# Attention scores and values of two feature tiles side by side in a gated decoder block

## The chip, the cores and the metric

One core of a Trainium2 chip runs one launch of the kernel. The metric is the device time of a launch in microseconds; lower is better. Before the change it is 444.75 us (median of three runs, 444.67 to 445.67).

## What is computed

The reference is one decoder block on 256 tokens of width 1024, in float32. Two mixers run beside each other on the same normalised input and are added with sigmoid gates; then come an output projection, a squared-ReLU MLP, a gated embedding and a final norm. The change touches only the attention mixer, which with 256 tokens and blocks of 256 is plain causal attention with a relative bias (cut to what matters):

```python
h = rms_norm(x, norm_mix_g[i])
za_u, za_v, q, k, v_att, g_a, g_b = jnp.split(h @ w_in[i], offsets, axis=-1)
y_a = sgu_mixer(jax.nn.gelu(za_u), jax.nn.gelu(za_v), ...)
s_own = jnp.einsum('bhqd,bhmd->bhqm', q_c, k_own) * scale + table[:, rel_bucket(dist_own)]
probs = jax.nn.softmax(jnp.where(dist_own >= 0, s_own, -jnp.inf))
y_b = jnp.einsum('bhqm,bhmd->bhqd', probs, v_own)        # 16 heads of 64 features
merged = jax.nn.sigmoid(g_a) * y_a + jax.nn.sigmoid(g_b) * y_b
x = x + merged @ w_out[i]
```

## The kernel before

Activations lie with features on the 128 partitions, in eight feature tiles of 128; a feature tile c holds the two heads 2c and 2c+1 (64 partitions each). All weights come as 53 tiles of 1 MB in one fixed order (`ORDER`, line 34). Each weight tile is split by two engines: ScalarE writes the rounded high part (`hi`, line 84), VectorE the remainder (`lo`, line 85). A projection is then three matmuls per 128x128 block (lines 117 to 119: hi with the high and the low half of the activations, lo with the high half), each 128x128 stationary and 256 columns moving. Of `hi` and `lo` there are three buffers each, and of the raw tiles four; `weights()` splits two tiles ahead of the one it hands out, so a tile is split while the two before it are used.

The schedule is by hand: each engine runs its instructions in the order in which the program issues them. The stretch around the change is the loop over J (two turns). A turn handles four feature tiles c to c+3 and eight weight tiles: keys for two tiles (`keys`, w_in 12+), attention's v (`proj_tok`, two w_va tiles), and the two sigmoid gates for two pairs of tiles (`proj_h(20..)` and `proj_h(24..)`, with `gate_tanh`). A projection is done in two halves of 24 matmuls, and its `mid` hook puts other TensorE work between the halves. The attention work per feature tile is:

- scores (lines 396 and 399): four matmuls, the two heads at once, each on 64 of the 128 rows of the array (tile 64x128), 256 or 128 columns. They are in full float32, so the chip runs each as two passes, and the profile counts eight.
- softmax: VectorE scales and adds the bias (lines 401, 403) and finds the maxima (line 407), ScalarE takes the exponentials (line 411). `att_normalise` (lines 418, 421) is VectorE's.
- `att_transpose` (line 430): six 128x128 transposes on TensorE, copied to `pt` by ScalarE (line 431).
- values (lines 441, 442): four matmuls, the two heads at once, each on 64 of the 128 columns of the array (tile 128x64), two passes each.
- when both tiles of a pair are done, `merge` (lines 451 to 454 on VectorE, then `split_act`: line 107 on ScalarE, line 108 on VectorE).

In the program before, every score tile and every value tile is put into the stream of projections at a place of its own: eight places for scores and eight for values, all with matmuls of 128x128 in front and behind. PSUM has one bank for `yb` (values), two buffers of two banks for scores, and three banks (`mm`) for projections and transposes together.

```python
        keys(b, mid=lambda: att_scores(c))
...
        ta[a] = gate_tanh(proj_h(20, a, transpose_and_score(c, c + 2)), f"ta{a}")
        att_normalise(c + 2)
        att_values(c)
        tb[a] = gate_tanh(proj_h(24, a, transpose_and_score(c + 1, c + 3)), f"tb{a}")
```

Of the kernel before, what the change touches and what calls it, by code (L numbers as in the profile page):

```python
# [10 lines left out]
F32 = mybir.dt.float32  # L11
# [5 lines left out]
P = 128  # L17
# [33 lines left out]
def block_kernel(ctx: ExitStack, tc: tile.TileContext, xt, xk, pt, rows, wst, bsp, rel, buckets, wts, out):  # L51
# [7 lines left out]
    scores = tc.tile_pool(name="scores", bufs=2, space=bass.MemoryType.PSUM)  # L59
    ps_scores = scores.__enter__()  # L60
# [34 lines left out]
    def weights(key, width, ahead=3):  # L95
        i = POS[key]
        split_to(i + ahead)
        k = 2048 // width
        return (hi[i].rearrange("p (k c) -> p k c", k=k), lo[i].rearrange("p (k c) -> p k c", k=k))


    def pair_tile(tag, name, k=KD):
        return act.tile([P, k, 2, S], F32R, tag=tag, name=name)
# [17 lines left out]
    def tok3(os_, x, wh, wl, first, last):  # L121

        ts = [slice(t * P, (t + 1) * P) for t in range(2)]
        for t in range(2):
            nc.tensor.matmul(os_[t], x[:, 0, ts[t]], wh, start=first, stop=False)  # L125
        for t in range(2):
            nc.tensor.matmul(os_[t], x[:, 0, ts[t]], wl, start=False, stop=False)  # L127
            nc.tensor.matmul(os_[t], x[:, 1, ts[t]], wh, start=False, stop=last)  # L128

    def halves(c):  # L130
        return slice(c * 512, (c + 1) * 512)

    def bank(tag="mm", bufs=3, shape=(P, 2, 256)):
        return ps.tile(list(shape), F32, tag=tag, name=f"{tag}_t", bufs=bufs)
# [80 lines left out]
    def proj_T(key, x, mid=None, ahead=3):  # L215

        wh, wl = weights(key, CW, ahead)
        o = bank()
        for f in range(2):
            fs = slice(f * P, (f + 1) * P)  # L220
            for k in range(KD):
                mm3(o[:, f], wh[:, k, fs], wl[:, k, fs], x[:, k], k == 0, k == KD - 1)
            if f == 0 and mid:
                mid()
        return o

    def proj_tok(name, c, x, mid=None):

        os_ = [bank(shape=(P, 512)) for t in range(2)]
        for i in range(2):  # L230
            wh, wl = weights((name, 2 * c + i), 512)
            for k in range(4):
                tok3(os_, x[:, 4 * i + k], wh[:, k], wl[:, k], i + k == 0, i == 1 and k == 3)
            if i == 0 and mid:
                mid()
        return os_
# [58 lines left out]
    hT = pair_tile("xA", "hT")  # L295
# [30 lines left out]
    o = proj_T(("w_in", 0), xg2, ahead=2)  # L326
# [4 lines left out]
    o = proj_T(("w_in", 1), xg2, ahead=2)  # L331
# [3 lines left out]
    o = proj_T(("w_in", 2), xg2, ahead=2)  # L335
# [3 lines left out]
    o = proj_T(("w_in", 3), xg2)  # L339
# [19 lines left out]
    def by_half(a):  # L359
        return a.rearrange("p c (t s) -> p (c t) s", t=2)  # L360
# [18 lines left out]
    for j in range(4):  # L379
        o = proj_T(("w_in", 8 + j), hT)  # L380
# [5 lines left out]

    va = act.tile([P, 2, D], F32, tag="t8a", name="va")
    mT = pair_tile("xB", "mT")
    sc_sb, pt_sb, yb = {}, {}, {}
    parts = (slice(0, 256), slice(256, 384))  # L390

    def att_scores(c):
        sp = ps_scores.tile([P, 2, 512], F32, tag="scores", name=f"sp{c}")
        for h in range(2):
            rs = slice(h * DH, (h + 1) * DH)
            nc.tensor.matmul(sp[:, h, 0:256], qT[rs, c, P:2 * P], kT[rs, c], start=True, stop=True)  # L396
        for h in range(2):
            rs = slice(h * DH, (h + 1) * DH)
            nc.tensor.matmul(sp[:, h, 256:384], qT[rs, c, 0:P], kT[rs, c, 0:P], start=True, stop=True)
        s = tmp.tile([P, 2, RVW], F32, tag="s", name=f"s{c}", bufs=3)  # L400
        nc.vector.scalar_tensor_tensor(s[:, :, 0:256], sp[:, :, 0:256], DH ** -0.5,
                                       TB[:, 2 * c:2 * c + 2, :], op0=OP.mult, op1=OP.add)
        nc.vector.scalar_tensor_tensor(s[:, :, 256:384], sp[:, :, 256:384], DH ** -0.5,
                                       TB[:, 2 * c:2 * c + 2, P:2 * P], op0=OP.mult, op1=OP.add)
        nm = small.tile([P, 2, 2], F32, tag="nm", name=f"nm{c}")
        for i, cs in enumerate(parts):
            nc.vector.tensor_reduce(nm[:, i], s[:, :, cs], axis=AX.X, op=OP.max, negate=True)  # L407
        sm = small.tile([P, 2, 2], F32, tag="sm", name=f"sm{c}")
        for i, cs in enumerate(parts):
            for h in range(2):  # L410
                nc.scalar.activation(s[:, h, cs], s[:, h, cs], AF.Exp, bias=nm[:, i, h:h + 1],  # L411
                                     accum_out=sm[:, i, h:h + 1])
        sc_sb[c] = (s, sm)

    def att_normalise(c):
        s, sm = sc_sb[c]
        rc = small.tile([P, 2, 2], F32, tag="rc", name=f"rc{c}")
        nc.vector.reciprocal(rc, sm)
        for i, cs in enumerate(parts):
            for h in range(2):  # L420
                nc.vector.tensor_scalar(s[:, h, cs], s[:, h, cs], rc[:, i, h:h + 1], 0.5,
                                        op0=OP.mult, op1=OP.mult)

    def att_transpose(c):
        s, _ = sc_sb.pop(c)
        pt_sb[c] = tmp.tile([P, 2, RVW], F32, tag="pt", name=f"pt{c}", bufs=2)
        for h in range(2):
            pp = bank(shape=(P, 512))
            for d, src in ((0, 256), (1, 0), (2, 128)):
                nc.tensor.transpose(pp[:, d * P:(d + 1) * P], s[:, h, src:src + P], ident)  # L430
            nc.scalar.activation(pt_sb[c][:, h], pp[:, :RVW], AF.Copy)

    def att_values(c):
        if c % 2 == 0:
            yb[c // 2] = bank("yb", 1)
        y = yb[c // 2][:, c % 2]
        pt_ = pt_sb.pop(c)
        for h in range(2):
            hs = slice((2 * c + h) * DH, (2 * c + h + 1) * DH)
            rs = slice(h * DH, (h + 1) * DH)  # L440
            nc.tensor.matmul(y[rs, :], va[:, 0, hs], pt_[:, h, 0:256], start=True, stop=False)  # L441
            nc.tensor.matmul(y[rs, P:2 * P], va[:, 1, hs], pt_[:, h, 256:384], start=False, stop=True)

    def gate_tanh(o, name):
        th = tmp.tile([P, 2, S], F32, tag="th", name=name, bufs=3)
        nc.scalar.activation(th, o, AF.Tanh, scale=0.5)
        return th

    def merge(j, ta, tb):
        cs = slice(2 * j, 2 * j + 2)  # L450
        nc.vector.scalar_tensor_tensor(ta, ta, 1.0, uT[:, cs], op0=OP.add, op1=OP.mult)
        nc.vector.scalar_tensor_tensor(by_half(tb), by_half(tb), 1.0, by_half(yb[j])[:, :, ::-1],
                                       op0=OP.add, op1=OP.mult)
        nc.vector.tensor_add(ta, ta, tb)
        split_act(mT[:, cs], ta)

    ta, tb = {}, {}

    def proj_h(c0, j, mid=None):
        return proj_T(("w_in", c0 + j), hT, mid=mid)  # L460

    def keys(j, mid=None):
        nc.scalar.activation(kT[:, 2 * j:2 * j + 2], proj_h(12, j, mid), AF.Copy)

    def transpose_and_score(c, nxt=None):
        def mid():
            att_transpose(c)
            if nxt is not None:
                att_scores(nxt)
        return mid  # L470

    def last_of(j):
        att_values(2 * j + 1)
        merge(j, ta[j], tb[j])

    for J in range(2):
        a, b, c = 2 * J, 2 * J + 1, 4 * J
        if J:
            last_of(a - 1)
        keys(a)  # L480
        keys(b, mid=lambda: att_scores(c))
        att_normalise(c)
        for t, o in enumerate(proj_tok("w_va", J, hT, mid=lambda: att_scores(c + 1))):
            nc.scalar.activation(va[:, t, halves(J)], o, AF.Copy)
        att_normalise(c + 1)
        ta[a] = gate_tanh(proj_h(20, a, transpose_and_score(c, c + 2)), f"ta{a}")
        att_normalise(c + 2)
        att_values(c)
        tb[a] = gate_tanh(proj_h(24, a, transpose_and_score(c + 1, c + 3)), f"tb{a}")
        att_normalise(c + 3)  # L490
        last_of(a)
        ta[b] = gate_tanh(proj_h(20, b, transpose_and_score(c + 2)), f"ta{b}")
        att_values(c + 2)
        tb[b] = gate_tanh(proj_h(24, b, transpose_and_score(c + 3)), f"tb{b}")


    xs1 = pair_tile("xA", "xs1")
# [10 lines left out]
    for i in range(3):  # L508
        wh, wl = weights(("w_out", i), 1024)
        for k in range(2):  # L510
            for o in range(KD):
                out_mm(i, k, o, wh, wl)
            if i + k == 0:
                last_of(3)

    def low_parts(pr):
        for k in (2 * pr, 2 * pr + 1):
# [290 lines left out]
```

## Time and profile before

| | |
|---|---|
| median of three runs | 444.75 us (444.67 to 445.67) |
| profiled execution, its own time | 444.61 us |
| span in its profile | 442.8 us |
| TensorE matmul busy | 426.8 us (96%), 2908 instructions |
| VectorE busy | 268.7 us (61%) |
| ScalarE busy | 225.6 us (51%) |
| TensorE share of the chain that ended last | 80% |
| mean granted TensorE clock | 0.991 of full speed |

Times inside the profile count from the start of the span. A TensorE row gives the start of a matmul and a modelled length; matmuls overlap, so what one costs the stream is the distance from its start to the start of the next, not its length. "PE" are matmuls, "PEld" weight loads, DVE is VectorE, ACT is ScalarE. A row "x4" merges four instructions of one line; its time is the start of the first. "mm_t" is whatever lies in the three shared PSUM banks, "sp" are scores, "yb_t" values, "s" the softmax tile, "pt" the transposed probabilities.

### The profile page before, as it was taken

To read this page: it belongs to the slowest core of one execution; us is meant where nothing else is said; L and a number is where in the kernel's file an instruction comes from. 1 tells how busy PE (TensorE), PEld (TensorE's weight loads), DVE (VectorE), ACT (ScalarE), POOL (GpSimd) and SP (SyncE) were. 2 spreads that over 40 slices of the span, in tenths; PEclk is the share of its full clock that TensorE was granted. 3 is DMA by queue.
4 is the path that set the end of the run, shared out by engine and by line. 5 is a ranking of instruction groups with operands and counts; after the bars stand their busy time and mean duration, and the time that the engine had idled before them with its cause. 6 is when DMAs were issued, how large, how long until landed. Compare 5 with 4: busy or idle time off the path is not lost.

```text
span 442.8 us, 6953 instructions
## 1 busy us (share of the span) xinstructions
PE 426.8 (96%) x2908; PEld 390.9 (88%) x2908; DVE 268.7 (61%) x359; ACT 225.6 (51%) x351; POOL 13.0 (3%) x21
## 2 busy tenths in 40 slices
PE   8999869999999999999999999999999999999992
PEld 7899669998999988999999999999999999888882
DVE  3757895464765757746466785555555555546554
ACT  5855424435745457454345564444444444434924
POOL 1010001000000000000000000000000000000012
PEclk9999989999999999999999999999999999999997
DMA  8998258644525345443541566555555555552002
GB/s 283 421 412 312 96 194 316 254 116 169 191 96 189 103 185 184 149 165 125 187 158 49 212 239 237 189 185 192 188 189 189 186 191 189 188 192 95 1 1 95
DMA packets 13408, 81.02 MB, mean 183 GB/s; under 512 B 1510, under 2 KB 1782, under 8 KB 4801
## 3 DMA queue, kind: packets, MB, share of 16 engines
q1 hardware_dynamic: 12240, 77.34, 48.2%
q0 software_dynamic: 848, 2.96, 1.9%
q8 instruction: 23, 0.38, 0.3%
q10 hardware_dynamic: 288, 0.27, 0.2%
q14 instruction: 9, 0.07, 0.0%
HBM read 79.49 MB, written 1.07 MB: 182 GB/s over the span
## 4 chain that ended last, share of the span: by engine, by line
PE 80%; DVE 4%; issue 2%; ACT 1%; POOL 0%; POOLq 0%; DVEq 0%
PE mm_t L117 14%; PE mm_t L118 14%; PE mm_t L119 14%; PE y L125 7%; PE y L128 7%; PE y L127 7%; PE mm_t L125 2%; PE mm_t L127 2%; PE mm_t L128 2%; DVE lo L85 2%; PE mm_t L430 1%; PE sp L396 1%; PE acc L117 1%; PE yb_t L441 1%; PE mm_t L666 1%
## 5 line engine op out<-in xcount | busy, mean ns | idle before, releaser
L85 DVE TENSOR_TENSOR lo<-raw,hi 128x1024 fp32r<-128x1024 f32 (+1 forms) x140 | 162.8, 1205 | 65.0 <-ACT hi L84 64.6
L84 ACT ACTIVATE hi<-raw 128x1024 fp32r<-128x1024 f32 (+1 forms) x140 | 138.1, 1036 | 39.3 <-issue 29.1
L117 PE MATMUL mm_t<-hT,hi 128*128 128x256 f32 x256 | 75.1, 294 | 3.3 <-ACT hT L107 3.3
L119 PE MATMUL mm_t<-hT,lo 128*128 128x256 f32 x256 | 73.1, 286 | 0.7 <-DVE lo L85 0.7
L118 PE MATMUL mm_t<-hT,hi 128*128 128x256 f32 x256 | 73.2, 286 | 0.3 <-DVE hT L108 0.3
L118 PE MATMUL mm_t<-xs,hi 128*128 128x256 f32 x256 | 72.7, 284 | 0.4 <-DVE xs L114 0.4
L117 PE MATMUL mm_t<-xs,hi 128*128 128x256 f32 x256 | 72.5, 283 | 0.0
L119 PE MATMUL mm_t<-xs,lo 128*128 128x256 f32 x256 | 72.5, 283 | 0.0
L117 PEld LDWEIGHTS mm_t<-hT,hi 128*128 128x128 f32 x256 | 49.6, 194 | 6.1 <-ACT hT L107 3.5
L119 PEld LDWEIGHTS mm_t<-hT,lo 128*128 128x128 f32 x256 | 49.7, 194 | 0.9 <-DVE lo L85 0.9
L118 PEld LDWEIGHTS mm_t<-hT,hi 128*128 128x128 f32 x256 | 49.7, 194 | 0.6 <-DVE hT L108 0.5
L118 PEld LDWEIGHTS mm_t<-xs,hi 128*128 128x128 f32 x256 | 48.9, 191 | 1.1 <-DVE xs L114 0.6
L117 PEld LDWEIGHTS mm_t<-xs,hi 128*128 128x128 f32 x256 | 49.0, 191 | 0.4
L119 PEld LDWEIGHTS mm_t<-xs,lo 128*128 128x128 f32 x256 | 48.9, 191 | 0.0
L545 ACT ACTIVATE r<-mm_t 128x512 f32<-128x512 f32 x16 | 9.5, 592 | 46.1 <-PE mm_t L119 46.1
L547 DVE TENSOR_TENSOR q<-r 128x512 f32<-128x512 f32 x16 | 11.0, 690 | 36.0 <-ACT r L545 36.0
L411 ACT ACTIVATE s<-s,nm 128x256 f32<-128x256 f32 (+1 forms) x32 | 14.2, 444 | 22.8 <-DVE nm L407 22.8
L128 PE MATMUL y<-hi,fs 128*128 128x512 f32 x64 | 24.9, 390 | 0.0
L127 PE MATMUL y<-lo,fs 128*128 128x512 f32 x64 | 24.9, 390 | 0.0
L125 PE MATMUL y<-hi,fs 128*128 128x512 f32 x64 | 19.8, 391 | 0.0
L119 PE MATMUL mm_t<-xg,lo 128*128 128x256 f32 x64 | 18.2, 284 | 1.6 <-DVE lo L85 1.6
L117 PE MATMUL acc<-mT,hi 128*128 128x256 f32 x64 | 18.2, 285 | 0.0
(195 smaller groups left out, 726.5 us busy)
## 6 DMA issues: line engine op xcount, KB each, us to landing
raw<-wts SPq DMA_DIRECT2D x67, 1024.0 KB, 4.9
TB<-rvd POOLq DMA_DIRECT2D x1, 2048.0 KB, 13.4
raw<-wts SPq DMA_DIRECT2D x4, 256.0 KB, 4.9
raw<-wts SPq DMA_DIRECT2D x2, 512.0 KB, 6.4
xtok<-xk SPq DMA_DIRECT2D x2, 512.0 KB, 10.0
sgu_b<-rows SPq DMA_DIRECT2D x2, 512.0 KB, 9.7
out<-ots SPq DMA_DIRECT2D x4, 256.0 KB, 2.0
xg<-xt SPq DMA_DIRECT2D x1, 512.0 KB, 7.1
```

What stands on the lines that cost most here:

```text
L84: nc.scalar.activation(hi[i][:, s], raw[i][:, s], AF.Copy)
L85: nc.vector.tensor_tensor(lo[i][:, s], raw[i][:, s], hi[i].bitcast(F32)[:, s], op=OP.subtract)
L117: nc.tensor.matmul(o, wh, x[:, 0], start=first, stop=False, **kw)
L118: nc.tensor.matmul(o, wh, x[:, 1], start=False, stop=False, **kw)
L119: nc.tensor.matmul(o, wl, x[:, 0], start=False, stop=last, **kw)
L125: nc.tensor.matmul(os_[t], x[:, 0, ts[t]], wh, start=first, stop=False)
L127: nc.tensor.matmul(os_[t], x[:, 0, ts[t]], wl, start=False, stop=False)
L128: nc.tensor.matmul(os_[t], x[:, 1, ts[t]], wh, start=False, stop=last)
L396: nc.tensor.matmul(sp[:, h, 0:256], qT[rs, c, P:2 * P], kT[rs, c], start=True, stop=True)
L411: nc.scalar.activation(s[:, h, cs], s[:, h, cs], AF.Exp, bias=nm[:, i, h:h + 1], accum_out=sm[:, i, h:h + 1])
L545: nc.scalar.activation(r, o, AF.Relu)
L547: nc.vector.tensor_mul(q2, r, r)
```

## The change

Scores are issued for two feature tiles in one go (`score_two`), and so are values (`value_two`); the matmuls of both tiles follow each other with nothing between them. `att_scores` is cut into its matmuls (`score_mm`) and the rest (`softmax`). Transposes stay one tile at a time, at other places: in a turn, tile c in the middle of the first gate projection, c+1 in the middle of the second (just ahead of the scores of c+2 and c+3), c+2 in the middle of the fourth, and c+3 after the fourth, between two projections. Values of the first pair go into the middle of the third gate projection, those of the second pair into the next turn's first `keys`, or into the output projection after the last turn.

```diff
-    def att_scores(c):
-        sp = ps_scores.tile([P, 2, 512], F32, tag="scores", name=f"sp{c}")
+    def score_mm(c):
+        sp = sp_[c] = ps_scores.tile([P, 2, 512], F32, tag="scores", name=f"sp{c}")
...
+    def softmax(c):
+        sp = sp_.pop(c)
...
+    def score_two(c):
+        for i in range(2):
+            score_mm(c + i)
+        for i in range(2):
+            softmax(c + i)
+
+    def value_two(j):
+        for i in range(2):
+            att_values(2 * j + i)
         merge(j, ta[j], tb[j])
+
+    def transpose_score(c):
+        att_transpose(c)
+        score_two(c + 1)
 
     for J in range(2):
         a, b, c = 2 * J, 2 * J + 1, 4 * J
-        if J:
-            last_of(a - 1)
-        keys(a)
-        keys(b, mid=lambda: att_scores(c))
+        keys(a, mid=(lambda: value_two(a - 1)) if J else None)
+        keys(b, mid=lambda: score_two(c))
         att_normalise(c)
-        for t, o in enumerate(proj_tok("w_va", J, hT, mid=lambda: att_scores(c + 1))):
+        att_normalise(c + 1)
+        for t, o in enumerate(proj_tok("w_va", J, hT)):
             nc.scalar.activation(va[:, t, halves(J)], o, AF.Copy)
-        att_normalise(c + 1)
-        ta[a] = gate_tanh(proj_h(20, a, transpose_and_score(c, c + 2)), f"ta{a}")
+        ta[a] = gate_tanh(proj_h(20, a, lambda: att_transpose(c)), f"ta{a}")
+        tb[a] = gate_tanh(proj_h(24, a, lambda: transpose_score(c + 1)), f"tb{a}")
         att_normalise(c + 2)
-        att_values(c)
-        tb[a] = gate_tanh(proj_h(24, a, transpose_and_score(c + 1, c + 3)), f"tb{a}")
         att_normalise(c + 3)
-        last_of(a)
-        ta[b] = gate_tanh(proj_h(20, b, transpose_and_score(c + 2)), f"ta{b}")
-        att_values(c + 2)
-        tb[b] = gate_tanh(proj_h(24, b, transpose_and_score(c + 3)), f"tb{b}")
+        ta[b] = gate_tanh(proj_h(20, b, lambda: value_two(a)), f"ta{b}")
+        tb[b] = gate_tanh(proj_h(24, b, lambda: att_transpose(c + 2)), f"tb{b}")
+        att_transpose(c + 3)
...
             if i + k == 0:
-                last_of(3)
+                value_two(3)
```

What moves, at three places. First TensorE in the middle of `keys(1)` of the first turn; before, only tile 0 stands there (sp0), and tile 1 stands in the middle of the v projection that follows:

```order
L119 MATMUL mm_t_941<-hT_309,lo13_802 128x256
L396 MATMUL sp0_966<-kT_608,qT_607 128x256 x2
L399 MATMUL sp0_966<-kT_608,qT_607 128x128 x2
L117 MATMUL mm_t_941<-hT_309,hi13_801 128x256
...
L128 MATMUL mm_t_1014<-hi14_877,hT_309 128x512
L396 MATMUL sp1_1047<-kT_608,qT_607 128x256 x2
L399 MATMUL sp1_1047<-kT_608,qT_607 128x128 x2
L125 MATMUL mm_t_1013<-hi15_935,hT_309 128x512
```

The same place now:

```order
L119 MATMUL mm_t_941<-hT_309,lo13_802 128x256
L396 MATMUL sp0_966<-kT_608,qT_607 128x256 x2
L399 MATMUL sp0_966<-kT_608,qT_607 128x128 x2
L396 MATMUL sp1_971<-kT_608,qT_607 128x256 x2
L399 MATMUL sp1_971<-kT_608,qT_607 128x128 x2
L117 MATMUL mm_t_941<-hT_309,hi13_801 128x256
```

Tile 1 follows tile 0 directly, and the v projection is left without a score tile in it.

Second, ScalarE's queue from there on, now (kT is the copy of the finished keys, hi16 the weight tile of the first gate projection; before, the two rows of s1 stood behind hi16):

```order
L414 ACTIVATE s0_976,sm0_982<-s0_976,nm0_979 128x256 x2
L414 ACTIVATE s0_976,sm0_982<-s0_976,nm0_979 128x128 x2
L414 ACTIVATE s1_987,sm1_993<-s1_987,nm1_990 128x256 x2
L414 ACTIVATE s1_987,sm1_993<-s1_987,nm1_990 128x128 x2
L466 ACTIVATE kT_608<-mm_t_941 128x512
L84 ACTIVATE hi16_1039<-raw16_799 128x1024 x2
L84 ACTIVATE hi17_1071<-raw17_875 128x1024 x2
```

The exponentials of the second tile now stand ahead of the key copy and of the next weight tile.

Third, TensorE between the last gate projection of the first turn and the first projection of the second, now (before, the values of tile 3 stood here, and the transposes of tile 3 in the middle of the projection):

```order
L119 MATMUL mm_t_1368<-hT_309,lo19_1176 128x256
L433 MATMUL mm_t_1431<-ident_106,s3_1238 128x128 x3
L433 MATMUL mm_t_1436<-ident_106,s3_1238 128x128 x3
L117 MATMUL mm_t_1449<-hT_309,hi20_1289 128x256
L118 MATMUL mm_t_1449<-hT_309,hi20_1289 128x256
```

Two of the three shared banks go to the transposes of tile 3 (1431, 1436, the banks that the transposes of tile 2 leave), and the next projection (1449) gets the bank of the projection that has just ended (1368).

## Rows read from the trace of the kernel before

**Rows 1.** Busy time by stretch: us; busy and instructions of PE, PEld, DVE, ACT, POOL; clock; DMA

```profile
96.20:149.30 53.10, 53.10 (x400) 48.10 (x400) 35.18 (x60) 30.09 (x64) 0.00 (x0) 1.00 0.40 139
```

**Rows 2.** Timeline of PE around the scores of tile 0: start, us, what

```profile
96.03 0.28 PE L119 MATMUL mm_t<-hT,lo 128*128 128x256 f32 x1
96.24 0.70 PE L396 MATMUL sp<-kT,qT 64*128 64x256 f32 x4
96.78 0.39 PE L399 MATMUL sp<-kT,qT 64*128 64x128 f32 x4
97.10 0.39 PE L117 MATMUL mm_t<-hT,hi 128*128 128x256 f32 x1
97.32 0.28 PE L118 MATMUL mm_t<-hT,hi 128*128 128x256 f32 x1
97.44 0.28 PE L119 MATMUL mm_t<-hT,lo 128*128 128x256 f32 x1
```

**Rows 3.** Timeline of PE, narrow windows: the second passes of the same scores

```profile
96.56 0.38 PE L396 MATMUL sp<-kT,qT 64*128 64x256 f32 x2
...
96.89 0.28 PE L399 MATMUL sp<-kT,qT 64*128 64x128 f32 x2
```

**Rows 4.** Timeline of PE around the values of tile 0

```profile
119.41 0.28 PE L119 MATMUL mm_t<-hT,lo 128*128 128x256 f32 x1
119.62 0.66 PE L441 MATMUL yb_t<-pt,va 128*64 128x256 f32 x4
120.10 0.40 PE L442 MATMUL yb_t<-pt,va 128*64 128x128 f32 x4
120.42 0.39 PE L117 MATMUL mm_t<-hT,hi 128*128 128x256 f32 x1
120.65 0.28 PE L118 MATMUL mm_t<-hT,hi 128*128 128x256 f32 x1
```

**Rows 5.** Tiles sp and yb: ns shortest/median/longest, first and last start (us), shapes

```profile
L396 PE MATMUL sp<-kT,qT x32: 376/428/480, 96.2 to 180.7; 64*128 64x256 f32 x32
...
L441 PE MATMUL yb_t<-pt,va x32: 379/404/431, 119.6 to 202.2; 128*64 128x256 f32 x32
```

**Rows 6.** Chain that ended last: six transposes in a gate projection

```profile
132.00 0.66 PE mm_t L430 x6
```

**Rows 7.** Timelines of PE and ACT: end of the first turn's last gate projection, its tanh

```profile
142.63 0.28 PE L119 MATMUL mm_t<-hT,lo 128*128 128x256 f32 x1
...
143.00 0.60 ACT L446 ACTIVATE tb<-mm_t 128x512 f32<-128x512 f32 x1 [2.32 <-PE mm_t L119]
```

**Rows 8.** Timeline of DVE: softmax of tile 0, then the next lo tile

```profile
97.38 0.68 DVE L401 SCALAR_TENSOR_TENSOR s<-sp,TB 128x512 f32<-128x512 f32 x1
...
98.31 1.00 DVE L407 TENSOR_REDUCE nm<-s 128x2 f32<-128x512 f32 x2
...
102.35 2.36 DVE L85 TENSOR_TENSOR lo<-raw,hi 128x1024 fp32r<-128x1024 f32 x2 [0.20 <-ACT hi L84]
```

**Rows 9.** Timeline of ACT: exponentials of tile 0 begin; the key copy behind them

```profile
99.02 0.51 ACT L411 ACTIVATE s<-s,nm 128x256 f32<-128x256 f32 x1 [1.70 <-DVE nm L407]
...
100.79 0.57 ACT L463 ACTIVATE kT<-mm_t 128x512 f32<-128x512 f32 x1
```

**Rows 10.** Timeline of PE: first reader of that lo tile

```profile
112.31 0.28 PE L119 MATMUL mm_t<-hT,lo 128*128 128x256 f32 x1
```

**Rows 11.** ACT, after the values of a pair: the merge's high part

```profile
145.29 0.63 ACT L107 ACTIVATE mT<-ta 128x512 fp32r<-128x512 f32 x1 [1.69 <-DVE ta L454]
```

**Rows 12.** DVE, the merge's product with the values

```profile
143.84 0.69 DVE L452 SCALAR_TENSOR_TENSOR tb<-tb,yb_t 128x512 f32<-128x512 f32 x1 [3.75 <-PE yb_t L442]
```

**Rows 13.** Timeline of ACT in the output projection: hi tiles

```profile
211.60 2.01 ACT L84 ACTIVATE hi<-raw 128x1024 fp32r<-128x1024 f32 x2 [3.75 <-issue]
217.36 2.01 ACT L84 ACTIVATE hi<-raw 128x1024 fp32r<-128x1024 f32 x2 [3.75 <-issue]
```

**Rows 14.** Timeline of PEld, narrow window: the next weights of the same values

```profile
119.88 0.15 PEld L442 LDWEIGHTS yb_t<-pt,va 128*64 128x64 f32 x2
```

More of the change, by code (lines that the diff above doesn't have):

```diff
@@ L388, in block_kernel @@
     mT = pair_tile("xB", "mT")
-    sc_sb, pt_sb, yb = {}, {}, {}
+    sp_, sc_sb, pt_sb, yb = {}, {}, {}, {}
     parts = (slice(0, 256), slice(256, 384))
-    def att_scores(c):
-        sp = ps_scores.tile([P, 2, 512], F32, tag="scores", name=f"sp{c}")
+    def score_mm(c):
+        sp = sp_[c] = ps_scores.tile([P, 2, 512], F32, tag="scores", name=f"sp{c}")
         for h in range(2):
@@ L463, in keys @@
         nc.scalar.activation(kT[:, 2 * j:2 * j + 2], proj_h(12, j, mid), AF.Copy)
[L465 to L473, printed above, removed]
+    def score_two(c):
[6 more added lines that the diff above has]
+            att_values(2 * j + i)
         merge(j, ta[j], tb[j])
+    def transpose_score(c):
+        att_transpose(c)
+        score_two(c + 1)
     for J in range(2):
         a, b, c = 2 * J, 2 * J + 1, 4 * J
-        if J:
-            last_of(a - 1)
-        keys(a)
-        keys(b, mid=lambda: att_scores(c))
+        keys(a, mid=(lambda: value_two(a - 1)) if J else None)
+        keys(b, mid=lambda: score_two(c))
         att_normalise(c)
-        for t, o in enumerate(proj_tok("w_va", J, hT, mid=lambda: att_scores(c + 1))):
+        att_normalise(c + 1)
+        for t, o in enumerate(proj_tok("w_va", J, hT)):
             nc.scalar.activation(va[:, t, halves(J)], o, AF.Copy)
-        att_normalise(c + 1)
-        ta[a] = gate_tanh(proj_h(20, a, transpose_and_score(c, c + 2)), f"ta{a}")
+        ta[a] = gate_tanh(proj_h(20, a, lambda: att_transpose(c)), f"ta{a}")
+        tb[a] = gate_tanh(proj_h(24, a, lambda: transpose_score(c + 1)), f"tb{a}")
         att_normalise(c + 2)
-        att_values(c)
-        tb[a] = gate_tanh(proj_h(24, a, transpose_and_score(c + 1, c + 3)), f"tb{a}")
         att_normalise(c + 3)
-        last_of(a)
-        ta[b] = gate_tanh(proj_h(20, b, transpose_and_score(c + 2)), f"ta{b}")
-        att_values(c + 2)
-        tb[b] = gate_tanh(proj_h(24, b, transpose_and_score(c + 3)), f"tb{b}")
+        ta[b] = gate_tanh(proj_h(20, b, lambda: value_two(a)), f"ta{b}")
+        tb[b] = gate_tanh(proj_h(24, b, lambda: att_transpose(c + 2)), f"tb{b}")
+        att_transpose(c + 3)
     xs1 = pair_tile("xA", "xs1")
```

## The prediction

> **What bounds the kernel now.** I read the busy shares by stretch first, because the change touches only the two turns of the loop, about 96 to 203 us of the span. In 96.2 to 149.3 us, the first turn, TensorE is busy for all of the 53.10 us at a granted clock of 1.00, which is its higher level (2.4 GHz), while VectorE has 35.18 and ScalarE 30.09 us of work [rows 1]. So nothing waits on TensorE's side: the turn lasts as long as the starts of its matmuls take, one after the other, and the question is what each start costs. For that I went to TensorE's timeline at one place of each kind.
>
> In the stream of projections a matmul starts 0.12 us after the one before (97.32 to 97.44) [rows 2]. From the last projection matmul ahead of the scores (96.03) to the second behind them (97.32) it is 1.29 us [rows 2]. Without the scores these two steps would take 0.24, so one visit to the scores costs **1.05 us**. The passes explain only part of that. The two heads run side by side, so a tile has four steps. The second pass of the wide pair holds the array for 0.22 us (96.56 to 96.78), the first of the narrow pair for 0.11 (96.78 to 96.89) [rows 2, 3]. Two wide and two narrow steps at this pace are **0.65 us**. The other 0.40 lies at the edges, where the stream changes from tiles of 128x128 to 64x128 and back: 0.09 going in (0.21 instead of 0.12), 0.10 in the first wide step (0.32 instead of 0.22), 0.10 going out (0.21 from 96.89 to 97.10, instead of 0.11), 0.10 in the first projection matmul (0.22 instead of 0.12) [rows 2, 3].
>
> Values show the same edges: from 119.41 to 120.65 it is 1.24 us, less 0.24 is **1.00 us**, and with steps of the same widths as the scores (256 and 128 columns, two passes each) 0.65 of that is the passes [rows 4]. 0.35 us are edges. All eight visits of each kind are alike: 32 records of each wide line with hardly any spread beyond the two passes (376 to 480 and 379 to 431 ns) [rows 5].
>
> **The change part by part.** Nothing is added or removed on any engine: the same matmuls, softmaxes, transposes and merges are issued in another order.
>
> *Scores.* Eight visits become four of two tiles. The second tile of a visit brings its four steps (0.65 us) but no edge of its own. This boundary, 64x128 behind 64x128 with another tile's weights, isn't in the trace. Its bounds are a full pair of edges (0.40, nothing saved) and none. The nearest row is the step from the wide to the narrow pair inside a tile, which also brings new weights in the same shape, and it has no edge (0.22 us) [rows 2, 3]. So I take none: 4 x 0.40 = 1.6 us saved.
>
> *Values.* Likewise 4 x 0.35 = 1.4 us; bounds 0 and 1.4, with the same choice. A value visit is 128x64 throughout.
>
> *Transposes* keep their number, and they are tiles of 128x128: six take 0.66 us, which is six narrow steps of 0.11 without an edge [rows 6]. Moving them costs nothing by itself. One of the moved ones makes a new wait. Tile 3's now stand between two projections, and the next projection gets the PSUM bank that the last one is just leaving. Its tanh on ScalarE starts 0.37 us after the last matmul's start (142.63 to 143.00) and takes 0.60, so the bank comes free at +0.97; TensorE, with 0.12 and 0.66 us of transposes, is there at +0.78 [rows 6, 7]. That is **0.2 us** of waiting, once: after the second turn the next matmuls write the banks of the scores. Bounds: 0 and 0.3.
>
> *Softmax, two in a row.* VectorE takes 1.93 us from the first score read to the last maximum (97.38 to 99.31) [rows 8], ScalarE 1.77 for one tile's exponentials (99.02 to 100.79) [rows 9]. They pipeline, so the second tile puts the key copy and the next weight tile about 2.0 us later: the lo tile that is done at 104.71 (102.35 and 2.36) [rows 8] is done near 106.7. Its first reader is at 112.31, about 0.4 earlier now [rows 10]. Cover: 5.2 us. I cost it at nothing; without that cover the price is whatever goes over. The loads that SP issues when that raw tile is read shift with it, and are for the tile four places on. In the second half of a turn a pair's softmax likewise ends long before its transposes, a projection and a half later. The place in the v projection where tile 1 was is gone, so ScalarE is freer there.
>
> *Sum.* 1.6 + 1.4 - 0.2 = 2.8 us. The profiled execution took 444.61 us, so 441.8; the median of the runs shown is 0.14 higher. I predict **441.9 us**. What is late next is nothing new: TensorE's own steps still set the pace.
>
> **Rivals.**
>
> *New weights wait at the second tile.* The second tile may pay the way in again (0.09 and 0.10 us) though not the way out. With up to 0.19 for each of eight second tiles, 1.5 us of the gain goes: 443.4 us. Against it: inside a value visit the loads for the narrow pair run from 119.88, while the wide pair, which uses the same rows of the array, still streams: the narrow pair's first matmul is at 120.10 [rows 4, 14]. By the Trainium skill, "TensorE: Matmul & The Clock Gate", section "The mechanism" of Part 3, a weight load overlaps running matmuls only when it is for another row group. By that rule this rival would hold, and the sum would be 1.3 instead of 2.8. The row just named speaks against the rule here.
>
> *The change doesn't do what it says:* edges belong to a tile and not to a change of shape. Then nothing is saved and the time stays at 444.6 to 444.8. The steps inside a visit speak against it.
>
> *The gain is given back later.* In the output projection the chain leaves TensorE, and ScalarE stands idle for 3.75 us ahead of a hi tile. If that wait ended on a load that comes when it comes, up to all of it would be lost: about 444.5. Against it: two such waits follow each other by 5.76 us, which is exactly 48 matmuls of 0.12 [rows 13]. ScalarE there follows TensorE, and moves up with it.
>
> *Slower: a new queue behind the merge.* The values of tiles 2 and 3 now stand in the middle of the second turn's first keys projection. ScalarE meets the merge's high part first, and the key copy queues behind it; the scores in the middle of the next projection need that copy. Say e is the start of that first projection. Values end at e + 2.88 + 1.65 = 4.5 (half a projection is 24 steps of 0.12; a value visit is now 1.00 + 0.65). In the worst order VectorE then has a whole lo tile (2.36) [rows 8], three merge steps of 0.69 [rows 12], and ScalarE 0.63 for the high part [rows 11] and 0.57 for the copy [rows 9]: 5.6 us, so the keys are ready at e + 10.1. The scores come at e + 3 x 2.88 + 1.65 = 10.3. So it decides only once those 5.6 us are over 5.8, and loses all the gain at 8.6. Were every step half as long again and a tile more in front, 10.8 us, TensorE would wait 5.0: 446.8. For it: after packing, the trace has two tiles arriving at once. By the Trainium skill, "TensorEngine Tiling (Array Packing)", section "PSUM Bottleneck", the copies out of PSUM can become the limit once TensorE is faster. Against it: those engines have over a third of the turn free [rows 1].
>
> **How the numbers follow.** 0.3%, 1.3 us, is about what a measurement of this kernel can tell from no change. Forecast 0.80; weights wait at the second tile 0.08 (half of it within 0.3%); nothing saved 0.04; given back 0.05; slower 0.03. So faster 0.84, same 0.13, slower 0.03. The range takes the forecast's own bounds (441.6 without the bank wait, less the scatter of runs) and the first rival: 441.3 to 443.4.
>
> **What would show it.** Right: eight places instead of sixteen where TensorE's steps change shape; in them the second tile's four steps in 0.65 us; wide records of the second tile all of the short kind; a wait of some 0.2 us behind the transposes of tile 3; no other wait of TensorE in the two turns; the first matmul of the output projection 2.8 us earlier and everything after it by as much. Wrong: the second tile's first step at 0.32 us (first rival), or a wait of TensorE on the key copy, on a lo tile or on s.

## The result, and the profile after

The changed kernel takes **442.38 us** (median of 4 runs, 442.29 to 442.8). The kernel before, run again beside it, took 445.2 us (4 runs, 444.67 to 445.67). The ratio is 0.9938 with an interval of 0.9924 to 0.9951: faster by about 0.6%, twice the 0.3% that the prediction took for what a measurement can tell from no change. The profiled execution took 442.39 us, against 444.61 before.

The engines' work is the same as before; only TensorE's busy time fell, by 2.2 us. Busy time, share of the span and instructions of each engine, changed kernel:

```profile
PE 424.6 (96%) x2908; PEld 391.2 (89%) x2908; DVE 268.6 (61%) x359; ACT 225.9 (51%) x351; POOL 13.1 (3%) x21
```

To size the gain without what lies outside the change, I take one stretch of TensorE's timeline in both kernels: from the last matmul of the spatial mixer (the one ahead of the first keys projection) to the last matmul of the output projection. First the kernel before, then the changed one (start, us, what; the first row's matmul starts 0.03 us after the mixer's last):

```profile
87.44 0.36 PE L117 MATMUL mm_t<-hT,hi 128*128 128x256 f32 x1
...
222.87 0.28 PE L119 MATMUL acc<-mT,lo 128*128 128x256 f32 x1
```

```profile
87.78 0.36 PE L117 MATMUL mm_t<-hT,hi 128*128 128x256 f32 x1
...
220.70 0.28 PE L119 MATMUL acc<-mT,lo 128*128 128x256 f32 x1
```

The stretch was 135.46 us and is 132.95 us (starts in ns, differences rounded): **2.52 us** shorter. Behind it both executions have 219.9 us to the end of the span. Ahead of it the changed kernel's execution happened to begin 0.34 us later, which is why its profiled time is 2.2 us lower and not 2.5. The medians of the two, each over four runs, are 2.8 us apart. That this is just the forecast's 2.8 is luck: the four runs of a kernel lie up to 1.0 us apart, and the stretch, which does not have this scatter, gives 2.52.

**Scores.** TensorE's timeline at the place of [rows 2], two tiles now; the row of x4 holds both heads and both passes:

```profile
96.38 0.28 PE L119 MATMUL mm_t<-hT,lo 128*128 128x256 f32 x1
96.59 0.70 PE L396 MATMUL sp<-kT,qT 64*128 64x256 f32 x4
97.12 0.39 PE L399 MATMUL sp<-kT,qT 64*128 64x128 f32 x4
97.34 0.60 PE L396 MATMUL sp<-kT,qT 64*128 64x256 f32 x4
97.78 0.39 PE L399 MATMUL sp<-kT,qT 64*128 64x128 f32 x4
98.09 0.39 PE L117 MATMUL mm_t<-hT,hi 128*128 128x256 f32 x1
98.32 0.28 PE L118 MATMUL mm_t<-hT,hi 128*128 128x256 f32 x1
```

The first tile's wide pair holds the array for 0.53 us (96.59 to 97.12), the second's for 0.44 (97.34 to 97.78): the 0.1 us at the way in is paid by the first tile alone. The first narrow pair hands over to the second tile in 0.22 (97.12 to 97.34, two steps of 0.11), while the second narrow pair needs 0.32 (to the ns) to the next projection matmul (97.78 to 98.09). So the boundary between the tiles has no edge. From 96.38 to 98.32 it is 1.94 us; two visits of one tile would take 2 x 1.285 and one base pair of steps (0.24) less, 2.33. A pair saves **0.39 us**.

**Values**, at the place that answers to [rows 4]:

```profile
129.22 0.28 PE L119 MATMUL mm_t<-hT,lo 128*128 128x256 f32 x1
129.43 0.66 PE L444 MATMUL yb_t<-pt,va 128*64 128x256 f32 x4
129.92 0.40 PE L445 MATMUL yb_t<-pt,va 128*64 128x128 f32 x4
130.13 0.65 PE L444 MATMUL yb_t<-pt,va 128*64 128x256 f32 x4
130.57 0.44 PE L445 MATMUL yb_t<-pt,va 128*64 128x128 f32 x4
130.94 0.39 PE L117 MATMUL mm_t<-hT,hi 128*128 128x256 f32 x1
131.16 0.28 PE L118 MATMUL mm_t<-hT,hi 128*128 128x256 f32 x1
```

It is 1.93 us (to the ns, from 129.22 to 131.16), where two visits would take 2 x 1.239 - 0.24 = 2.24: a pair saves **0.31 us**. The boundary again costs nothing (129.92 to 130.13 is 0.21), but the end does: the second narrow row is 0.44 long where the first is 0.40, and the way out from it is 0.37 (130.57 to 130.94) where it was 0.32 in [rows 4]. From the second tile's second pass on the other head's matmuls start 57 ns behind the first head's; in the first tile it is 13 ns. The array is left that 0.04 us later. The weight loads show where it begins, in all four visits alike: in the second tile the other head's first load starts 0.11 us behind the first head's (130.03 and 130.14 in this visit), in the first tile 0.01.

All four visits of each kind agree with these to 0.01 us. The wide records of the two tiles (shortest, median, longest in ns; first and last start), which answer to [rows 5]:

```profile
L396 PE MATMUL sp<-kT,qT x32: 376/377/480, 96.6 to 178.1; 64*128 64x256 f32 x32
...
L444 PE MATMUL yb_t<-pt,va x32: 379/379/430, 129.4 to 200.0; 128*64 128x256 f32 x32
```

The medians have moved from the middle (428 and 404) to the short kind: only a quarter of the records, instead of half, still carry the way in.

**The bank.** TensorE behind the transposes of tile 3, and ScalarE's tanh of the projection ahead of them:

```profile
140.19 0.28 PE L119 MATMUL mm_t<-hT,lo 128*128 128x256 f32 x1
140.31 0.82 PE L433 MATMUL mm_t<-ident,s 128*128 128x128 f32 x6
141.22 0.39 PE L117 MATMUL mm_t<-hT,hi 128*128 128x256 f32 x1
141.44 0.28 PE L118 MATMUL mm_t<-hT,hi 128*128 128x256 f32 x1
...
195.45 0.82 PE L433 MATMUL mm_t<-ident,s 128*128 128x128 f32 x6
196.03 0.36 PE L117 MATMUL acc<-mT,hi 128*128 128x256 f32 x1
```

```profile
140.57 0.60 ACT L449 ACTIVATE tb<-mm_t 128x512 f32<-128x512 f32 x1 [2.32 <-PE mm_t L119]
```

Between the transposes' first start and the next projection lie 0.91 us in the first turn (140.31 to 141.22) and 0.58 in the second (195.45 to 196.03), where the next matmuls write other banks. The tanh ends at 141.17, and the projection starts 0.05 later. The step into it is 0.364 us instead of 0.029, the one behind it 0.223 instead of 0.202: 0.36 us in all. The view of waits for TensorE between 86 and 215 us is empty: this one shows only as a long step.

### The profile page after: what moved, and what is told of

Its sections match the earlier page's. It is cut to its first block, busy times and chain, and to the rows that moved or that the text cites. A ratio compares the mean times of both kernels' runs of the same rounds, so it can differ in the third digit from the quotient of the medians.

```text
span 440.6 us, 6948 instructions
## 1 busy us (share of the span) xinstructions
PE 424.6 (96%) x2908; PEld 391.2 (89%) x2908; DVE 268.6 (61%) x359; ACT 225.9 (51%) x351; POOL 13.1 (3%) x21
## 4 chain that ended last, share of the span: by engine, by line
PE 80%; DVE 4%; issue 2%; ACT 1%; POOL 0%; POOLq 0%; DVEq 0%; ACTq 0%
PE mm_t L117 14%; PE mm_t L118 14%; PE mm_t L119 14%; PE y L125 7%; PE y L128 7%; PE y L127 7%; PE mm_t L125 2%; PE mm_t L127 2%; PE mm_t L128 2%; DVE lo L85 2%; PE acc L117 1%; PE mm_t L671 1%; PE mm_t L433 1%; PE mm_t L670 1%; PE mm_t L672 1%
```

## Experiments

The kernel before ran beside each group of these: 444.85 us (20 runs, e1 to e4), 445.35 (10 runs, e5 to e8), 444.95 (13 runs, e9). They are shown in the order e1 to e9; the last three, shown together, are e7 with 12, e8 with 24 and e9 with 18 additions. "Stretch" is the one defined above; it comes from the profiled execution.

**The change again, as it is.**

> The changed kernel as it is, for comparison on the same chip as the next three. Against the kernel before: edges theory (a change of tile shape on TensorE costs about 0.2 us, a visit of scores 0.40 in edges, one of values 0.35, eight visits fewer, one new bank wait of 0.25): 2.75 us less. Rival of the queues (the gain comes from the freer ScalarE and VectorE): the same number, so this run does not tell them apart.

442.69 us (442.45 to 443.15), ratio 0.9948 (0.9936 to 0.996); stretch 132.94. The stretch came back to 1 ns, while the total moved by 0.3 us. So parts can be compared by the stretch much more finely than by the time.

**Scores paired, values one by one.** Values of the pair's first tile stand in the middle of the projection, those of the second behind it.

```diff
+    def last_of(j):
+        att_values(2 * j + 1)
         merge(j, ta[j], tb[j])
...
-        keys(a, mid=(lambda: value_two(a - 1)) if J else None)
+        keys(a, mid=(lambda: att_values(c - 2)) if J else None)
+        if J:
+            last_of(a - 1)
...
-        ta[b] = gate_tanh(proj_h(20, b, lambda: value_two(a)), f"ta{b}")
+        ta[b] = gate_tanh(proj_h(20, b, lambda: att_values(c)), f"ta{b}")
+        last_of(a)
```

> Scores two tiles at a time as in the change, values one tile at a time again (8 visits). Edges theory: 4 x 0.40 saved, 0.25 for the bank behind the transposes of tile 3 stays: 1.35 us less than before, 1.4 more than the change. Rival of the queues: the softmaxes, which are what fills VectorE and ScalarE, stand as in the change, so nearly all of the 2.75 us should be there.

443.61 us (443.17 to 444.45), ratio 0.9973 (0.9963 to 0.9984); stretch 134.09, 1.37 shorter than before. Pairing the values is therefore worth the other 1.15 of the 2.52, and undoing it leaves the bank wait (a step of 0.364 again).

**Values paired, scores one by one.** A score tile again stands in the middle of `keys(b)`, of the v projection and of the second gate projection, and one behind it.

```diff
-        keys(b, mid=lambda: score_two(c))
+        keys(b, mid=lambda: score_one(c))
...
+        for t, o in enumerate(proj_tok("w_va", J, hT, mid=lambda: score_one(c + 1))):
...
         tb[a] = gate_tanh(proj_h(24, a, lambda: transpose_score(c + 1)), f"tb{a}")
+        score_one(c + 3)
```

> Values two tiles at a time as in the change, scores and softmax one tile at a time again (8 visits; one of them is back in the v projection). Edges theory: 4 x 0.35 saved less 0.25 for the bank: 1.15 us less than before, 1.6 more than the change. Rival of the queues: about nothing is saved, since the softmaxes are spread as before.

444.13 us (443.6 to 445.16), ratio 0.9981 (0.9971 to 0.999); stretch 134.63, only 0.84 shorter than before. The expectation took 0.35 for a value pair and 0.25 for the bank wait. With the measured 4 x 0.306 and 0.36 it is 0.86. Both experiments hold the bank wait: their gains, 1.37 and 0.84, and the 0.36 that is in them once too often make 2.57, against the change's 2.52, so the two halves hardly touch each other. The rival of the queues falls with the two: it wanted nearly the whole gain from the first (1.37 came) and about none from the second (0.84).

**A transpose between the two score tiles.** It brings the change of shape back while the scores stay paired in place and in number.

```diff
     def transpose_score(c):
+        score_mm(c + 1)
         att_transpose(c)
-        score_two(c + 1)
+        score_mm(c + 2)
+        for i in range(2):
+            softmax(c + 1 + i)
```

> The change with one thing moved: the six transposes of tile c+1 stand between the two score tiles instead of in front of them (two places in the whole program; the same instructions, the stream of projections is left no more often). Edges theory: 128x128 transposes between two 64x128 tiles make four edges of two, so 2 x 0.40 = 0.8 us more than the change, and the second score tile's first wide step is 0.32 us again there. Rival: what costs is leaving and entering the stream of projections: 0.0 us more. Second rival (the way in hangs on new weights): the second tile's first step was already 0.22 in the change, so nothing more to lose there.

443.16 us (442.51 to 444.27), ratio 0.996 (0.9946 to 0.9974); stretch 133.65, 0.71 longer than the change's. TensorE's timeline at the first of its two places:

```profile
122.57 0.70 PE L396 MATMUL sp<-kT,qT 64*128 64x256 f32 x4
123.10 0.39 PE L399 MATMUL sp<-kT,qT 64*128 64x128 f32 x4
123.42 0.88 PE L433 MATMUL mm_t<-ident,s 128*128 128x128 f32 x6
124.23 0.70 PE L396 MATMUL sp<-kT,qT 64*128 64x256 f32 x4
124.76 0.39 PE L399 MATMUL sp<-kT,qT 64*128 64x128 f32 x4
125.08 0.39 PE L117 MATMUL mm_t<-hT,hi 128*128 128x256 f32 x1
```

The second tile's wide pair is 0.53 us again (124.23 to 124.76), and both narrow pairs pay 0.32 to get out. Four steps grew: out of the scores (0.20 instead of 0.11), within the first transposes (0.17 instead of 0.11), back in (0.20 instead of 0.11) and the first wide step (0.32 instead of 0.22), 0.35 for each place and 0.71 for two. What is paid is the change of shape: had an edge belonged to a tile, or to leaving the stream of projections, this kernel would have been as fast as the change.

**No projection behind tile 3's transposes.** Tile 2's transposes join the values in the third gate projection, tile 3's take their place in the fourth.

```diff
-        ta[b] = gate_tanh(proj_h(20, b, lambda: value_two(a)), f"ta{b}")
-        tb[b] = gate_tanh(proj_h(24, b, lambda: att_transpose(c + 2)), f"tb{b}")
-        att_transpose(c + 3)
+        ta[b] = gate_tanh(proj_h(20, b, lambda: value_transpose(a, c + 2)), f"ta{b}")
+        tb[b] = gate_tanh(proj_h(24, b, lambda: att_transpose(c + 3)), f"tb{b}")
```

> The change, but tile c+2 is transposed right behind the values of the first pair and tile c+3 in the middle of the last gate projection, so that no transposes stand between two projections; the merge is issued behind the transposes. Theory: the wait on the bank that the tanh still reads (in the changed kernel the step is 0.36 instead of 0.03 us, and 0.36 us in all) is gone and nothing else changes: 0.36 us less than the change, 133 - 0.4 = 132.6 us from the last spatial-mixing matmul to the last matmul of the output projection. Rival (the step is the price of transposes between two projections, whatever the bank): the same, since no transposes stand there any more. It is told apart by e2 to e4, where transposes stand between two projections in the second turn too, without the bank, and take no longer.

442.29 us (441.68 to 443.4), ratio 0.9928 (0.9911 to 0.9944); stretch 132.53, 0.41 shorter than the change's (0.36 expected; the other 0.05 was not followed up), and the long step is gone. Nor was it the weights that were late: the same projection now starts 53.17 us into the stretch, behind an ordinary step of 0.12, where it started at 53.47. The wait is the bank's, and it is gone with the place.

**Values and scores in one place.** A pair's values go straight ahead of the next pair's scores, transposes one tile at a time in the other projections; the tanh tiles have four buffers instead of three, since a gate now waits longer for its merge.

```diff
+    def value_score(j, c):
+        if j >= 0:
+            att_values(2 * j)
+            att_values(2 * j + 1)
+        score_two(c)
...
+        keys(a, mid=(lambda: att_transpose(c - 1)) if J else None)
+        keys(b, mid=lambda: value_score(a - 1, c))
+        if J:
+            merge(a - 1, ta[a - 1], tb[a - 1])
...
+        tb[a] = gate_tanh(proj_h(24, a, lambda: att_transpose(c + 1)), f"tb{a}")
+        ta[b] = gate_tanh(proj_h(20, b, lambda: value_score(a, c + 2)), f"ta{b}")
...
+        tb[b] = gate_tanh(proj_h(24, b, lambda: att_transpose(c + 2)), f"tb{b}")
+        merge(a, ta[a], tb[a])
```

> Values of one pair and scores of the next in one visit (128x64 tiles directly behind which 64x128 tiles follow), three times; transposes alone in the middle of projections; no bank wait; one buffer more for the tanh tiles, so that the merge can come later. Theory: an edge belongs to a change of shape, so 128x64 to 64x128 is one edge of about 0.2 us, where the change has two (0.4): 3 x 0.2 and the bank's 0.36, 0.95 us less than the change (132.0 us for the same stretch). Rival (an edge belongs to a shape being set up and to its being torn down, so two small shapes behind each other cost two): 0.36 less, 132.6.

**441.57 us** (441.18 to 441.81), ratio 0.9913 (0.9899 to 0.9928); stretch 131.99, 0.95 shorter than the change's. It is the fastest of all and beats both kernels: by the ratio its interval just touches the changed kernel's, by the stretch the distance is plain. TensorE where the values end and the scores begin:

```profile
128.25 0.65 PE L444 MATMUL yb_t<-pt,va 128*64 128x256 f32 x4
128.69 0.44 PE L445 MATMUL yb_t<-pt,va 128*64 128x128 f32 x4
129.06 0.70 PE L396 MATMUL sp<-kT,qT 64*128 64x256 f32 x4
129.59 0.39 PE L399 MATMUL sp<-kT,qT 64*128 64x128 f32 x4
```

From 128x64 to 64x128 there is one edge: the way out 0.37 (128.69 to 129.06), the wide pair 0.53 (129.06 to 129.59). The whole visit is 3.44 us; a pair of values and a pair of scores apart would be 1.93 + 1.94 - 0.24 = 3.63. Three such visits save 3 x 0.19, and the bank wait is gone (0.36): 0.93 of the 0.95. The run also bears on another rival: scores and values run as two passes each and projections as one, so an edge might have belonged to the number of passes. Here both neighbours have two passes, and the edge is there.

**How much cover the softmaxes have.** Behind the pair's two softmaxes at the first place of each turn, VectorE does additions into a tile that nothing reads any more, 12, 24 and 18 of them.

```diff
             softmax(c + i)
+        for i in range(12 if c % 4 == 0 else 0):
+            nc.vector.tensor_tensor(dg, TB[:, 0:2, 0:P], TB[:, 2:4, 0:P], op=OP.add)
```

> The change with 12 additional VectorE additions of 128x256 (about 0.33 us each, 4.0 us, into a tile that nobody reads) behind the softmax of the first pair of each turn. Theory: the first reader of the next lo tile comes 5.3 us after that tile is done, so 4.0 us in front of it cost nothing: as the change, within 0.1 us in the two turns. Rival (VectorE is already at its limit when two softmaxes come at once): 4.0 us per turn, 8 in all.

> The same with 24 additions, 7.9 us. Theory: 7.9 less the cover of 5.3 and the 0.7 us in which VectorE waits there now anyway, so TensorE waits 1.9 to 2.6 us for the lo tile in each turn: 3.8 to 5.3 us more than the change. Rival: 16 us more. A second rival (all of it is hidden, since other tiles can wait too): nothing more.

> Between the last two: 18 additions, which in those two runs took 0.46 us each and not 0.33, so 8.3 us. What holds the first reader is the first half of the lo tile: with 12 additions that half ended 1.9 us before its reader. Theory: 6 more additions (2.75 us) turn that into a wait of 0.9 us per turn, 1.8 us more than the change in the two turns if TensorE's granted clock stays at 1.00, which it did not after the waits of 3.5 us. Rival (the 11.7 us of the run with 24 additions are all proportional to the additions): 8.8 us more than the change.

With 12 (5.48 us, 0.46 each): 442.19 us (441.76 to 443.28), ratio 0.9933 (0.9911 to 0.9955); stretch 132.945, as long as the change's. With 18 (8.23 us): 445.11 us (444.01 to 445.55), ratio 0.9995 (0.9983 to 1.0008); stretch 134.90, 1.96 longer. With 24 (11.01 us): 454.56 us (451.46 to 454.94), ratio 1.0191 (1.0161 to 1.0221); stretch 144.66, 11.72 longer, where 3.8 to 5.3 were expected. TensorE's view of waits, first with 18, then with 24 additions (us in total, times, longest):

```profile
PE mm_t L119 <- DVE lo L85: 1.4, 2, 0.7
```

```profile
PE mm_t L119 <- DVE lo L85: 7.0, 2, 3.5
```

It is the lo tile's first reader that waits, in either turn. With 18, the two steps are 1.03 and 0.97 us instead of 0.12, 1.76 of the 1.96. The other 0.2 is in the step behind each (114.25 to 114.47 in the first turn): 0.22 instead of 0.12, as long as the step in the first projection matmul behind scores or values. With 24, they are 3.80 and 3.74, 7.3 us; about 2 us more than at most expected. An addition took 0.46 us and not the 0.33 that the expectation took, which is 3.1 us more in a turn; that the cover was longer than expected (below) takes back about a third of it. The other 4.4 us is in the stretches behind the waits (columns as in [rows 1]; 24 additions):

```profile
112.60:116.50 3.90, 0.39 (x4) 0.18 (x2) 3.83 (x13) 2.64 (x4) 0.00 (x0) 1.00 0.00 0
116.50:121.60 5.10, 5.10 (x30) 5.10 (x31) 5.10 (x5) 0.52 (x2) 0.00 (x0) 0.67 0.56 199
116.40:117.80 1.40, 1.37 (x11) 1.37 (x12) 1.40 (x2) 0.00 (x0) 0.00 (x0) 1.00 0.00 0
118.20:121.20 3.00, 3.00 (x16) 3.00 (x16) 3.00 (x4) 0.24 (x1) 0.00 (x0) 0.50 0.80 279
176.90:180.00 3.10, 3.10 (x14) 3.10 (x15) 3.10 (x3) 0.00 (x0) 0.00 (x0) 0.50 0.34 66
180.00:184.00 4.00, 4.00 (x25) 4.00 (x25) 2.47 (x3) 0.98 (x2) 0.00 (x0) 0.65 1.01 420
```

TensorE is idle for all but 0.39 of 3.90 us. Behind that it works on at a granted clock of 1.00 (116.4 to 117.8) and is then at 0.50, the lower level of 1.2 GHz (118.2 to 121.2); the mean of the 5.1 us from 116.5 is 0.67. Behind the second wait it is at 0.50 from the start (176.9 to 180.0), and 0.65 on the mean of the next 4.0 us: 5.1 x 0.33, 3.1 x 0.50 and 4.0 x 0.35 are 4.6 us lost, near the 4.4 that are missing. With 18 additions, behind idle stretches of 0.9 us, the granted clock stays 1.00 through both turns.

## Why the prediction was right

The forecast case held: the time is inside the range, and its sign and mechanism are as said. By its steps:

- **Scores, 1.6 us:** 4 x 0.389 = 1.56. The choice to take the boundary without an edge, from the step between the wide and the narrow pair of one tile, was right, and the transpose between the tiles shows why: the edge goes with the shape. By the Trainium skill, "TensorEngine Tiling (Array Packing)", section "Key Properties", a change of the tiling mode drains TensorE, and a change of the tile alone does not; the 0.11 us of the boundary and the 0.35 of the transpose put back between agree with it.
- **Values, 1.4 us:** 4 x 0.306 = 1.22. Here the term was mis-sized. It took the second tile as four steps of the first tile's pace; the second head's matmuls trail by 57 ns instead of 13 and leave the array 0.04 us later, in each of four visits. Of the second tile's loads only the other head's first waits for a semaphore in all four visits (ScalarE's, whose copy to `pt` had ended more than 2.5 us before), and in score pairs, where no load of the second tile waits, the heads stay 7 ns apart. No run took that wait away, so the cause stays open.
- **Bank wait, 0.2 us:** 0.36, once, as placed. The prediction freed the bank at the tanh's end; the projection started 0.05 us behind that, and its next step was 0.02 longer. The tanh itself started 0.38 behind the last matmul, as in [rows 7]. TensorE also came to it earlier than reckoned: by starts six transposes take 0.57 us to the next projection (five steps of 0.109 and one of 0.029, as in the second turn above), not the 0.66 of the chain's row [rows 6]. Its upper bound of 0.3 was just passed.
- **Two softmaxes in a row, nothing:** right. The lo tile, which is done at 106.90, has 5.3 us to its first reader (5.2 forecast); the reader waits for its first half, done at 105.8 (the first of the two rows that are merged here, 1.23 us), so the cover that counts is 6.4 us. The additions bear that out. With 18 the lo tile starts at 112.98, in an execution whose stretch starts 1.15 later, which is a delay of 7.3; less 6.4 it is the 0.9 that the reader waits. (7.3 and not 8.23, since the additions first fill 0.7 us in which VectorE was idle ahead of the lo tile.) With 12 the lo tile starts at 108.96, a delay of 4.5, and nothing waits. The lo tile and its reader in the changed kernel, VectorE and TensorE:

```profile
104.54 2.36 DVE L85 TENSOR_TENSOR lo<-raw,hi 128x1024 fp32r<-128x1024 f32 x2 [0.21 <-ACT hi L84]
...
112.20 0.28 PE L119 MATMUL mm_t<-hT,lo 128*128 128x256 f32 x1
```

- **Not in the sum:** about 0.1 us. In the kernel before, the 512-column matmuls of the v projection stepped at up to 0.236 us behind the score tile in its middle and at 0.227 elsewhere; without the score tile only its first few steps are that long. Why is open.

Together 1.56 + 1.22 - 0.36 + 0.10 = 2.52 us, the stretch's own difference. The forecast of 2.8 was 0.3 too high: 0.2 in the values and 0.2 in the bank wait, less the 0.1 that was not in it. The median came out 0.5 above the forecast of 441.9; the other 0.2 is less than the part ahead of the stretch scatters by (below).

**The rivals.** *New weights wait at the second tile* fell: its first wide step is 0.22 and not 0.32 us, and the boundary 0.11. By the Trainium skill, "TensorE: Matmul & The Clock Gate", section "The mechanism" of Part 3, weights load beside running matmuls only for another row group; here the second tile's weights come for the same rows and cost no step, so the measurement decides against that sentence. *Edges belong to a tile* fell with the change itself, whose second tiles have none, and again with the transpose between. *Given back later* fell: behind the last matmul of the output projection every one of the eleven profiled executions has 219.9 us to the end. *A queue behind the merge* did not come: in the second turn the key copy still waits for TensorE, not TensorE for it, and is done at 149.56, 2.2 us ahead of the scores that read it (151.73). ScalarE, changed kernel:

```profile
147.34 0.63 ACT L107 ACTIVATE mT<-ta 128x512 fp32r<-128x512 f32 x1 [3.51 <-DVE ta L457]
...
148.96 0.60 ACT L466 ACTIVATE kT<-mm_t 128x512 f32<-128x512 f32 x1 [0.99 <-PE mm_t L119]
```

The last three experiments do not try that queue. They show the same kind of wait at another place, a late lo tile: it decides once 6.4 us of delay are used up, and with waits of 3.5 us it costs more than the wait.

## What to carry to other kernels

Where TensorE's starts bound a stretch, count the places where the shape of its tiles changes, and read from the timeline what one such change costs (here about 0.2 us): side by side, work of one shape pays it once, and work of two small shapes may share one too. Look for the moved step that lands between two users of one bank; it shows as a long step and not in the view of waits. Before moving work of another engine together, reckon the cover to the first half of the tile that comes late, not to the whole of it, and compare small changes by a stretch between two fixed instructions.

## What was not expected of the hardware

**A long wait can be paid twice.** Behind an idle stretch of 3.5 us in the middle of full ones, TensorE's granted clock fell to 0.50, in one place after 1.4 us of work at 1.00, while in the other it was at 0.50 when the work began; in the two places together 4.4 us more were lost. Behind idle stretches of 0.9 us it stayed at 1.00. Where between the two it turns was not tried. The second payment does not seem to be the same each time: of the four runs with 24 additions one took 451.46 us at a mean granted clock of 0.986, the others 454.43 to 454.94 at 0.977, and only one of these was profiled.

**The scatter of this kernel's time has a place.** Busy time by stretch, 50 to 70 us (columns as in [rows 1]), ahead of everything that was changed; first the changed kernel, then the one with the transposes between:

```profile
50.00:70.00 20.00, 15.71 (x108) 14.34 (x108) 16.83 (x20) 10.58 (x13) 1.78 (x2) 0.91 0.52 184
```

```profile
50.00:70.00 20.00, 15.90 (x101) 14.42 (x100) 15.96 (x19) 9.73 (x13) 1.78 (x2) 0.83 0.51 175
```

In the eleven profiled executions this stretch has a granted clock of 0.91 (five of them, and the first keys projection then starts at 87.4 to 88.0 us) or of 0.83 (six, 88.3 to 89.2 us). Which of the two comes does not seem to go with the edit: the order of the work up to there is the same in all, and the runs of the kernel before alone go from 444.34 to 446.17 us (20 runs, e1 to e4). It moves a run by about 1 us, while the stretch behind it repeats to 0.01 us in the three executions that have the change's order on TensorE and no new wait (the changed kernel, e1 and e7).
